# Every third low part of the weight units on GpSimd, from the differential heads' query projection to the first output projection

## The chip, the core and the metric

The kernel runs on one core of a Trainium2 chip. A core has five engines with queues of their own, each of which takes its instructions strictly in order: TensorE (PE in the profile, with its weight loads as PEld), VectorE (DVE), ScalarE (ACT), GpSimd (POOL) and SyncE (SP, which here only issues DMAs). The metric is the device time of one execution in microseconds; less is better. The time before is the median of three runs.

## The reference, cut to what matters

Two blocks of two layers each run on 256 tokens of width 1024. Only the first layer of the first block is touched by the change:

```
proj = h @ w_in                          # w_in: 1024 x 4096
qa, ka, va, qb, kb, vb, g = split(proj)  # 512 columns each, g has 1024
ya = dilated_mixture_attention(qa, ka, va)          # 8 heads
yb = differential_attention(qb, kb, vb, lam, ...)   # 4 heads, two softmaxes each
y  = concat(ya, yb) * silu(g)
x  = x + gate * (y @ w_out)              # w_out: 1024 x 1024
```

`gate` belongs to layer 0; `shift`, `scale` and `gate` of layer 1 are products of one vector `cs` with 1024 x 3072 weights (`ada_w`), and the kernel forms them during layer 0.

## The kernel before, in words

All matrix products are made in three passes on pairs of numbers: an f32 value is split into a high part, rounded to TensorE's reduced f32 format, and a low part, the rest. `mm3` (lines 245, 246, 247) issues the three matmuls high by high, low by high and high by low. The activations are split once. The weights are streamed: `unit` (line 224) loads 128 partitions by 1024 f32 (512 KB) into a raw tile `wr` by SP, ACT casts it to the high part `wh` (line 227), and DVE subtracts it from the raw tile to form the low part `wl` (line 228). There are 3 raw, 5 high and 5 low buffers (`NR, NH, NL`), so the load of the fourth unit from here waits until the `wl` of this one is formed, and SP, in order, holds all later loads behind it.

A projection of 512 columns takes four units, the output projection (`out_proj`) eight. In layer 0 the order is: qa, ka, va in two halves, twelve units; then the softmax of the `ya` heads (`scores_a`, `values_a`); then qb, kb, vb, the first half of the gate (`sgT_done`), the second half (columns 3584 on, below: the second gate projection), and the output projection, 28 units together. Softmax needs DVE on the path to TensorE: DVE adds bias to the scores in PSUM and takes the least (line 398), ACT exponentiates (401), DVE scales the probabilities (line 678 for `ya`, 731 for `yb`), TensorE transposes them (410). For `yb` GpSimd raises the variance to a power (`rstd`, line 337) and DVE applies it (751); at the end DVE multiplies `yb` by the gate (579) and TensorE transposes it (582) for the last half of the output projection.

Between all this lies the vector by matrix product for `ada_w`: `part` loads 256 KB pieces `aw` by SP (line 517), DVE multiplies and adds each into `macc` (462 for the first of eight, then 464), GpSimd adds one row of bias to one partition of `macc` (line 519), and TensorE sums over partitions (523).

The written order fixes priorities. A scheduler that runs when the program is built sets the order of the instructions on each engine, with costs of its own for each instruction. What an engine will do next is thus fixed before the run, and an instruction that isn't ready holds all behind it.

Of the kernel before, what the change touches and what calls it, by code (L numbers as in the profile page):

```python
# [9 lines left out]
F32 = mybir.dt.float32  # L10
# [89 lines left out]
class Net:  # L100
    def __init__(self, ctx, tc, a):
        self.tc, self.nc, self.a = tc, tc.nc, a
        p = lambda name, bufs, **k: ctx.enter_context(tc.tile_pool(name=name, bufs=bufs, **k))
        self.p_const = p("const", 1)
        self.p_raw = p("raw", NR)
        self.p_hi = p("whi", NH)
        self.p_lo = p("wlo", NL)
        self.p_act = p("act", 2)
        self.p_g = p("gat", 5)
        self.p_big = p("big", 2)  # L110
        self.p_ng = p("ng", 1)
        self.p_par = p("par", 3)
        self.ph = {}
        self.p_col = p("colp", 22)
        self.p_mm = p("mm", 4, space=PSUM)
        self.p_mx = p("mx", 4, space=PSUM)
        self.load_consts()
# [99 lines left out]
    def unit(self, src, shape, pieces=1):  # L217

        nc = self.nc
        raw = self.p_raw.tile([128, 1024], F32, name="wr", tag="raw")  # L220
        hi = self.p_hi.tile([128, 1024], F32R, name="wh", tag="hi")
        lo = self.p_lo.tile([128, 1024], F32R, name="wl", tag="lo")
        v = (lambda t: t) if len(shape) == 1 else v2
        nc.sync.dma_start(v(raw), src)
        m = 1024 // pieces
        for i in range(0, 1024, m):
            nc.scalar.copy(hi[:, i:i + m], raw[:, i:i + m])  # L227
            nc.vector.tensor_sub(lo[:, i:i + m], raw[:, i:i + m], hi[:, i:i + m].bitcast(F32))  # L228
        return v(hi), v(lo)

    def block(self, w, c0, k0=0, k1=8, pieces=1):
# [188 lines left out]
def v2(t):  # L420
    return t.rearrange("p (a b) -> p a b", a=2)
# [130 lines left out]
def gated_out(n, act, w, gate, after):  # L552
    nc = n.nc

    def done(t, j, ps):
        s = slice(j * 512, j * 512 + 512)
        tmp = n.g2("go")
        nc.vector.tensor_mul(tmp, ps, gate[:, s])
        nc.vector.tensor_add(n.x[:, t, s], n.x[:, t, s], tmp)
    n.out_proj(act, w, done, after)  # L560


def pipelined(items, first, second, lag=2, after=None):

    got = []
    for i in range(items + lag):
        if i < items:
            got.append(first(i))
        if i >= lag:
            second(i - lag, got[i - lag])  # L570
            if after:
                after(i - lag)
# [25 lines left out]
def even_layer(n, mod, later, follow):  # L598
    nc, a = n.nc, n.a
# [4 lines left out]
    def fm_done(name, scale):  # L604
        def done(i, ps):
            t = n.s2(name)
            if scale is None:
                nc.scalar.copy(t, ps)
            else:
                nc.scalar.activation(t, ps, AF.Copy, scale=scale)  # L610
            fm[name, i] = v2(t)
        return done
# [61 lines left out]
    def values_a(pr, got):  # L674
# [7 lines left out]
        ya[pr] = n.s2("ya", tag="yp")  # L682
        nc.scalar.copy(ya[pr], ps)
    pipelined(4, scores_a, values_a, 1, later)
    n.proj_fm(act, w, 1536, fm_done("qb", -0.125))
    n.proj_fm(act, w, 2048, fm_done("kb", None))
    n.proj_tok(act, w, 2560, tok_done("vb"))
# [77 lines left out]
        pair_out(n, yb[h], [sg[1, 0], sg[1, 1]], h * 128, yT, 4 + h)  # L765
    following = follow()
    gated_out(n, yT, a["ab_w_out"][0], mod.gate, following.tile)
    return following


# [103 lines left out]
def first_block(n):  # L874
    nc = n.nc
    c = n.ccol("c", 0, 8)
    cs = n.p_const.tile([128, 8], F32, name="cs")
    nc.scalar.activation(cs, c, AF.Tanh, scale=0.5)
    nc.vector.scalar_tensor_tensor(cs, cs, 1.0, c, op0=OP.add, op1=OP.mult)
    nc.vector.tensor_scalar(cs, cs, 0.5, None, op0=OP.mult)  # L880
    n.cs = cs
    n.csB = n.ng("csB")
    nc.vector.tensor_copy(n.csB.rearrange("p (a b) -> p a b", a=8), bc(cs.unsqueeze(2), [128, 8, 128]))
    mods = [Mod(n, 0)]

    todo = [(0, 2, 0), (0, 2, 1), (1, 1, 0), (1, 1, 1), (1, 0, 0), (1, 0, 1), (1, 2, 0), (1, 2, 1)]
    open_ = []

    def later(i):

        if open_:
            open_.pop()()
        if i == 2:
            mods.append(Mod(n, 1))
        if i < len(todo):
            m, part, half = todo[i]
            open_.append(mods[m].part(part, half))
    ada = even_layer(n, mods[0], later, lambda: AdaNorm(n, mods[1]))
    return odd_layer(n, ada.act, mods[1], lambda i: later(6 + i),
                     lambda: DoubleNorm(n, "norm1_g_2", 0, mods[1].gate)).act  # L900
# [844 lines left out]
```

## Time and profile before

| | |
|---|---|
| median of 3 runs | 1309.55 us (1307.87 to 1313.42) |
| the profiled execution | 1304.1 us, of which the span is 1302.3 us |
| PE busy | 95% of the span |
| DVE busy | 65% of the span, 120.28 of the 147.00 us from 60 to 207 us |
| ACT busy | 49% |
| POOL busy | 5% |

The span is cut by the profile's own clock from the first to the last instruction. Times of rows are microseconds from the start of the span. An engine's busy share says only how long it was at work; what it waited for stands beside a row in square brackets, as the idle time just before it and what ended it.

### The profile page before, as it was taken

Reading aid. Unit: us, or ns where it says so; the run is one execution under the profiler, and the core shown is the slowest. Engines: PE = TensorE matmul, PEld = TensorE weight load, DVE = VectorE, ACT = ScalarE, POOL = GpSimd, SP = SyncE. Lnnn points to the kernel's source line nnn. Section 1 sums busy time; section 2 is a strip of 40 time slices with the busy share of each in tenths; the row PEclk is TensorE's granted clock in tenths of the full one; section 3 lists DMA queues with packets and bytes.
Section 4 is the critical chain, followed back from the end, with each engine's and each line's share of the span. In section 5 each row is a group of like instructions: output and inputs, shape, how many; then the busy total and the mean of one; then the engine's idle time right before and its main releaser. Section 6 shows DMA issues by size and latency. Waiting matters only on the chain.

```text
span 1302.3 us, 21332 instructions
## 1 busy us (share of the span) xinstructions
PE 1240.6 (95%) x8352; PEld 1047.7 (80%) x8352; DVE 851.2 (65%) x1456; ACT 644.0 (49%) x1083; POOL 68.9 (5%) x82
## 2 busy tenths in 40 slices
PE   6889889999899999999999999999999999999997
PEld 3767667977787777887899987987787887999986
DVE  6977888676658755766755544668755757655543
ACT  3454645685655345444644433556345444544432
POOL 0021120000101000000000000010000000000000
PEclk8999999999999999999999999999999999999999
DMA  8988865654553233465666654753242564766552
GB/s 315 325 274 277 257 197 172 202 179 122 178 170 98 84 114 98 149 210 162 196 186 185 181 192 129 234 149 96 82 128 83 177 196 130 226 183 188 180 192 81
DMA packets 104960, 227.25 MB, mean 175 GB/s; under 512 B 8206, under 2 KB 8350, under 8 KB 104860
## 3 DMA queue, kind: packets, MB, share of 16 engines
q1 hardware_dynamic: 102560, 219.18, 54.0%
q0 software_dynamic: 1984, 6.60, 1.8%
q8 instruction: 65, 1.06, 0.3%
q14 instruction: 35, 0.29, 0.1%
q10 hardware_dynamic: 316, 0.12, 0.0%
HBM read 224.82 MB, written 1.05 MB: 173 GB/s over the span
## 4 chain that ended last, share of the span: by engine, by line
PE 70%; DVE 7%; issue 5%; ACT 3%; DMA 2%; POOL 1%; POOLq 0%; DVEq 0%; ACTq 0%; SPq 0%
PE mm L246 20%; PE mm L245 19%; PE mm L247 19%; PE p L369 2%; DVE wl L228 2%; PE hs L1156 1%; ACT wh L227 1%; PE sc L376 1%; PE px L1440 1%; PE tr L324 1%; DMA wr<-in_gu_dram 1%; PE pv L385 1%; PE cm L376 1%; PE pt L410 1%; PE pv L1002 1%
## 5 line engine op out<-in xcount | busy, mean ns | idle before, releaser
L228 DVE TENSOR_TENSOR wl<-wr,wh 128x1024 fp32r<-128x1024 f32 (+1 forms) x372 | 431.3, 1165 | 268.6 <-ACT wh L227 266.5
L227 ACT CAST wh<-wr 128x1024 fp32r<-128x1024 f32 (+1 forms) x372 | 369.7, 1002 | 396.7 <-PE mm L247 164.7
L245 PE MATMUL mm<-hh,wh 128*128 128x256 f32 x1168 | 332.1, 286 | 1.0 <-ACT hh L328 0.9
L247 PE MATMUL mm<-hh,wl 128*128 128x256 f32 x1168 | 332.7, 285 | 0.0
L246 PE MATMUL mm<-hl,wh 128*128 128x256 f32 x1168 | 332.3, 285 | 0.0
L245 PEld LDWEIGHTS mm<-hh,wh 128*128 128x128 f32 x1168 | 224.4, 193 | 3.7 <-ACT hh L328 1.9
L247 PEld LDWEIGHTS mm<-hh,wl 128*128 128x128 f32 x1168 | 224.5, 192 | 2.1 <-issue 1.9
L246 PEld LDWEIGHTS mm<-hl,wh 128*128 128x128 f32 x1168 | 224.6, 192 | 1.5 <-issue 1.2
L246 PE MATMUL mm<-wl,hh 128*128 128x512 f32 (+1 forms) x448 | 178.3, 398 | 1.5 <-DVE wl L228 1.5
L245 PE MATMUL mm<-wh,hh 128*128 128x512 f32 (+1 forms) x448 | 177.3, 396 | 0.9 <-DVE ropet L1069 0.4
L247 PE MATMUL mm<-wh,hl 128*128 128x512 f32 (+1 forms) x448 | 175.5, 392 | 0.4 <-DVE hl L329 0.3
L246 PEld LDWEIGHTS mm<-wl,hh 128*128 128x128 f32 x448 | 85.0, 190 | 19.7 <-DVE wl L228 2.4
L245 PEld LDWEIGHTS mm<-wh,hh 128*128 128x128 f32 x448 | 84.9, 190 | 18.7 <-ACT hh L328 1.2
L247 PEld LDWEIGHTS mm<-wh,hl 128*128 128x128 f32 x448 | 84.8, 189 | 17.0 <-DVE hl L329 1.4
L245 PE MATMUL mm<-wh,ff 128*128 128x512 f32 x176 | 69.5, 395 | 0.0
L246 PE MATMUL mm<-wl,ff 128*128 128x512 f32 x176 | 69.5, 395 | 0.0
L247 PE MATMUL mm<-wh,ff 128*128 128x512 f32 x176 | 69.4, 395 | 0.0
L464 DVE SCALAR_TENSOR_TENSOR macc<-aw,cs,macc 128x512 f32<-128x512 f32 x78 | 58.4, 762 | 11.9 <-DMA aw<-in_ada_w_dram 11.5
L401 ACT ACTIVATE p<-p,nm 128x256 f32<-128x256 f32 (+1 forms) x80 | 39.7, 497 | 32.0 <-DVE nm L398 29.2
L246 PE MATMUL mm<-wl,yTh 128*128 128x512 f32 x128 | 50.6, 396 | 1.1 <-DVE wl L228 1.1
L247 PE MATMUL mm<-wh,yTl 128*128 128x512 f32 x128 | 50.0, 390 | 0.0
L245 PE MATMUL mm<-wh,yTh 128*128 128x512 f32 x128 | 49.4, 395 | 0.1
(388 smaller groups left out, 1533.7 us busy)
## 6 DMA issues: line engine op xcount, KB each, us to landing
wr<-in_w_in_dram SPq DMA_DIRECT2D x120, 512.0 KB, 3.8
wr<-in_gu_dram SPq DMA_DIRECT2D x88, 512.0 KB, 3.7
wr<-in_w_ffn_down_dram SPq DMA_DIRECT2D x44, 512.0 KB, 3.3
aw<-in_ada_w_dram SPq DMA_DIRECT2D x80, 256.0 KB, 3.9
wr<-in_ab_w_in_dram SPq DMA_DIRECT2D x32, 512.0 KB, 5.3
wr<-in_c_w_in_dram SPq DMA_DIRECT2D x20, 512.0 KB, 4.4
wr<-in_w_branch_dram SPq DMA_DIRECT2D x16, 512.0 KB, 3.2
wr<-in_w_out_dram SPq DMA_DIRECT2D x16, 512.0 KB, 3.2
```

What stands on the lines that cost most here:

```text
L227: nc.scalar.copy(hi[:, i:i + m], raw[:, i:i + m])
L228: nc.vector.tensor_sub(lo[:, i:i + m], raw[:, i:i + m], hi[:, i:i + m].bitcast(F32))
L245: mm(out, lhsT=ah, rhs=bh, start=start, stop=False, **kw)
L246: mm(out, lhsT=ah, rhs=bl, start=False, stop=False, **kw)
L247: mm(out, lhsT=al, rhs=bh, start=False, stop=stop, **kw)
L324: nc.tensor.transpose(ps[:, j * 128:(j + 1) * 128], src[:, (g + j) * 128:(g + j + 1) * 128], self.ident)
L369: self.nc.tensor.matmul(out[r], lhsT=lhsT[:, r], rhs=rhs, **kw)
L376: mm = lambda out, lhsT, rhs: self.nc.tensor.matmul(out, lhsT=lhsT, rhs=rhs, start=True, stop=True)
L385: mm = lambda hh, kc: self.nc.tensor.matmul(ps[HALF[hh], :], lhsT=vs(hh, kc), rhs=pTs[hh][:, kc * 256:kc * 256 + 256], start=(kc == 0), st ...
L401: nc.scalar.activation(p, p, AF.Exp, bias=nm, scale=-1.0, accum_out=l)
L410: nc.tensor.transpose(ps[:, kc * 256 + t * 128:kc * 256 + t * 128 + 128], p[:, t, kc * 128:kc * 128 + 128], self.ident)
L464: nc.vector.scalar_tensor_tensor(acc, w, n.cs[:, k:k + 1], acc, op0=OP.mult, op1=OP.add)
```

## The change: which engine forms the low part

A counter `shared` runs while layer 0 goes from the projection of qb to the end of the output projection. It starts at 1 and goes 2, 3, 1, 2, 3 ...; whenever it is 3, GpSimd takes the subtraction instead of DVE. The second unit of the 28 is the first to go there, then every third: 9 units. Elsewhere nothing changes in the text. (Line numbers of the changed kernel are 1 to 6 higher: its line 230 is 228 here, 522 is 519, 467 is 464, 340 is 337.)

```
@@ __init__
         self.p_lo = p("wlo", NL)
+        self.shared = 0
@@ unit
             nc.scalar.copy(hi[:, i:i + m], raw[:, i:i + m])
-            nc.vector.tensor_sub(lo[:, i:i + m], raw[:, i:i + m], hi[:, i:i + m].bitcast(F32))
+            self.shared = self.shared and self.shared % 3 + 1
+            (nc.gpsimd if self.shared == 3 else nc.vector).tensor_sub(
+                lo[:, i:i + m], raw[:, i:i + m], hi[:, i:i + m].bitcast(F32))
@@ even_layer
     pipelined(4, scores_a, values_a, 1, later)
+
+    n.shared = 1
     n.proj_fm(act, w, 1536, fm_done("qb", -0.125))
...
     gated_out(n, yT, a["ab_w_out"][0], mod.gate, following.tile)
+    n.shared = 0
     return following
```

The scheduler then orders DVE, PE, ACT, SP and POOL anew within layer 0; behind it the order is as it was. Three places follow.

GpSimd's queue from the unpacking of the masks (`msk`) to the second `rstd`, first before and then in the changed kernel. `lv`, `G1`, `sub` and `sk` are DMAs that it issues itself.

```order
L519 TENSOR_TENSOR macc_760<-macc_760,adab_785 1x512
L519 TENSOR_TENSOR macc_850<-macc_850,adab_875 1x512
L167 DMA lv_1488<-in_rows_dram 128x64 x4
L167 DMA G1_940<-in_rows_dram 128x1024
L167 DMA sub_1498<-in_rows_dram 128x128
L519 TENSOR_TENSOR macc_944<-macc_944,adab_969 1x512
L519 TENSOR_TENSOR macc_1000<-macc_1000,adab_1025 1x512
L519 TENSOR_TENSOR macc_1602<-macc_1602,adab_1627 1x512
L167 DMA sk_2384<-in_rows_dram 128x16
L337 TENSOR_TENSOR rstd_1595<-var_1593,mhalf_97 128x2
L519 TENSOR_TENSOR macc_1693<-macc_1693,adab_1718 1x512
L337 TENSOR_TENSOR rstd_1686<-var_1684,mhalf_97 128x2
```

```order
L230 TENSOR_TENSOR wl_1158<-wr_1156,wh_1157 128x1024
L522 TENSOR_TENSOR macc_850<-macc_850,adab_875 1x512
...
L230 TENSOR_TENSOR wl_1176<-wr_1174,wh_1175 128x1024
L522 TENSOR_TENSOR macc_944<-macc_944,adab_969 1x512
L168 DMA sub_1498<-in_rows_dram 128x128
L230 TENSOR_TENSOR wl_1296<-wr_1294,wh_1295 128x1024
L522 TENSOR_TENSOR macc_1000<-macc_1000,adab_1025 1x512
...
L230 TENSOR_TENSOR wl_1826<-wr_1824,wh_1825 128x1024
L340 TENSOR_TENSOR rstd_1595<-var_1593,mhalf_97 128x2
L522 TENSOR_TENSOR macc_1693<-macc_1693,adab_1718 1x512
L340 TENSOR_TENSOR rstd_1686<-var_1684,mhalf_97 128x2
L230 TENSOR_TENSOR wl_1844<-wr_1842,wh_1843 128x1024
```

Each moved subtraction has come in among work of GpSimd that was there before; the one of `wl_1844` (the last unit of the second gate projection) stands right behind the second `rstd`, and two more follow later, the third and the sixth unit of the output projection.

DVE's queue at the end of the second gate projection, before and in the changed kernel. `wl_1940` and `wl_1958` are the first two units of the output projection, `yb_1808` is the last head, `sg` the gate, `macc_2976` the last accumulation of `ada_w` that is formed in layer 0.

```order
L335 TENSOR_SCALAR var_1816<-ss_1809 128x2
L228 TENSOR_TENSOR wl_1844<-wr_1842,wh_1843 128x1024
L751 SCALAR_TENSOR_TENSOR yb_1808<-pv_1807,rstd_1818,sub_1498 128x128 x2
L464 SCALAR_TENSOR_TENSOR macc_2976<-aw_2992,cs_123,macc_2976 128x512
L228 TENSOR_TENSOR wl_1940<-wr_1938,wh_1939 128x1024
L464 SCALAR_TENSOR_TENSOR macc_2976<-aw_2995,cs_123,macc_2976 128x512
L549 SCALAR_TENSOR_TENSOR sg_1896<-th_1897,mm_1822 128x512
...
L579 TENSOR_TENSOR yb_1808<-yb_1808,sg_1900 128x128
L228 TENSOR_TENSOR wl_1958<-wr_1956,wh_1957 128x1024
```

```order
L338 TENSOR_SCALAR var_1791<-ss_1784 128x2
L230 TENSOR_TENSOR wl_1940<-wr_1938,wh_1939 128x1024
...
L756 SCALAR_TENSOR_TENSOR yb_1808<-pv_1807,rstd_1818,sub_1498 128x128 x2
L467 SCALAR_TENSOR_TENSOR macc_2976<-aw_2992,cs_123,macc_2976 128x512
L230 TENSOR_TENSOR wl_1958<-wr_1956,wh_1957 128x1024
L467 SCALAR_TENSOR_TENSOR macc_2976<-aw_2995,cs_123,macc_2976 128x512
L552 SCALAR_TENSOR_TENSOR sg_1896<-th_1897,mm_1822 128x512
...
L582 TENSOR_TENSOR yb_1808<-yb_1808,sg_1900 128x128
L230 TENSOR_TENSOR wl_1994<-wr_1992,wh_1993 128x1024
```

`wl_1844` has left DVE, `wl_1940` now stands ahead of the last two heads, and `wl_1958` is formed ahead of the gating of the heads instead of behind it.

SP's queue in the same stretch, before and in the changed kernel. `wr_1974` and `wr_1992` are the raw tiles of the third and fourth unit of the output projection.

```order
L224 DMA wr_1956<-in_ab_w_out_dram 128x1024
L517 DMA aw_2894<-in_ada_w_dram 128x512
L517 DMA aw_2897<-in_ada_w_dram 128x512
...
L517 DMA aw_2995<-in_ada_w_dram 128x512
L517 DMA aw_2998<-in_ada_w_dram 128x512
L224 DMA wr_1974<-in_ab_w_out_dram 128x1024
L224 DMA wr_1992<-in_ab_w_out_dram 128x1024
```

```order
L225 DMA wr_1956<-in_ab_w_out_dram 128x1024
...
L225 DMA wr_1974<-in_ab_w_out_dram 128x1024
L520 DMA aw_2980<-in_ada_w_dram 128x512
...
L520 DMA aw_2995<-in_ada_w_dram 128x512
L225 DMA wr_1992<-in_ab_w_out_dram 128x1024
L520 DMA aw_2998<-in_ada_w_dram 128x512
L225 DMA wr_2010<-in_ab_w_out_dram 128x1024
```

The third unit of the output projection is now loaded six `aw` pieces before the point where it stood behind all of them.

## Rows read from the trace of the kernel before

**Rows 1.** The page: busy us, share of the span and instructions of each engine.

```profile
PE 1240.6 (95%) x8352; PEld 1047.7 (80%) x8352; DVE 851.2 (65%) x1456; ACT 644.0 (49%) x1083; POOL 68.9 (5%) x82
```

**Rows 2.** Busy time of each engine, 60 to 207 us, granted clock, DMA share.

```profile
60.00:207.00 147.00, 128.49 (x731) 100.94 (x729) 120.28 (x270) 76.84 (x172) 25.15 (x25) 0.97 0.80 253
```

**Rows 3.** What PE waited for, 60 to 207 us: total, times, longest.

```profile
PE pt L410 <- DVE p L731: 6.1, 3, 3.4
PE pt L410 <- DVE p L678: 5.7, 4, 2.8
PE sc L376 <- DVE nm L398: 2.9, 1, 2.9
PE mm L246 <- DVE wl L228: 2.3, 3, 1.2
```

**Rows 4.** What DVE waited for in the same stretch, longest first.

```profile
DVE macc L464 <- DMA aw<-in_ada_w_dram: 10.9, 12, 3.8
DVE wl L228 <- ACT wh L227: 5.5, 7, 1.2
```

**Rows 5.** Busy time of line 228 alone on DVE, from the projection of qb on.

```profile
61.50:201.00 139.50, 34.08 (x28) 0.96 0.81 254
```

**Rows 6.** GpSimd's own operations: line 519's shortest, median and longest ns; and a cast.

```profile
L519 POOL TENSOR_TENSOR macc<-macc,adab x8: 1271/1460/2152, 72.4 to 183.6; 1x512 f32<-1x512 f32 x8
...
57.75 0.92 POOL L194 CAST msk<-mskf 128x896 uint8<-128x896 f32 x1 [4.00 <-DMA mskf<-in_msk_dram]
```

**Rows 7.** DVE and GpSimd in order of time, where line 519 ran: start, us, engine.

```profile
70.98 0.35 DVE L678 TENSOR_SCALAR p<-p,rl 128x256 f32<-128x256 f32 x1
72.71 1.38 DVE L678 TENSOR_SCALAR p<-p,rl 128x256 f32<-128x256 f32 x1
...
124.16 1.22 DVE L228 TENSOR_TENSOR wl<-wr,wh 128x1024 fp32r<-128x1024 f32 x1
125.30 0.42 DVE L398 CUSTOM_DVE_ANT_0 p<-sc,bias 128x256 f32<-128x256 f32 x1
125.72 1.36 DVE L464 SCALAR_TENSOR_TENSOR macc<-aw,cs,macc 128x512 f32<-128x512 f32 x1
...
138.73 2.15 POOL L519 TENSOR_TENSOR macc<-macc,adab 1x512 f32<-1x512 f32 x1 [12.20 <-PE mm L247]
155.62 1.29 POOL L519 TENSOR_TENSOR macc<-macc,adab 1x512 f32<-1x512 f32 x1 [7.80 <-PE mm L247]
155.89 1.30 DVE L462 TENSOR_SCALAR macc<-aw,cs 128x512 f32<-128x512 f32 x1 [0.26 <-DMA aw<-in_ada_w_dram]
157.23 0.75 DVE L464 SCALAR_TENSOR_TENSOR macc<-aw,cs,macc 128x512 f32<-128x512 f32 x1
159.03 0.88 DVE L731 SCALAR_TENSOR_TENSOR p<-p,rl 128x256 f32<-128x256 f32 x2
169.18 1.89 DVE L731 SCALAR_TENSOR_TENSOR p<-p,rl 128x256 f32<-128x256 f32 x2
170.99 0.47 DVE L462 TENSOR_SCALAR macc<-aw,cs 128x512 f32<-128x512 f32 x1
```

**Rows 8.** The cast of `wr_1842`, GpSimd's second `rstd`, the subtraction, SP's next loads.

```profile
160.05 1.05 ACT L227 CAST wh<-wr 128x1024 fp32r<-128x1024 f32 x1 [2.00 <-PE mm L246]
160.06 0.70 POOL L337 TENSOR_TENSOR rstd<-var,mhalf 128x2 f32<-128x2 f32 x1 [3.16 <-DVE var L335]
177.32 1.22 DVE L228 TENSOR_TENSOR wl<-wr,wh 128x1024 fp32r<-128x1024 f32 x1
178.61 15.00 SPq L224 DMA_DIRECT2D wr<-in_ab_w_out_dram  x6
```

**Rows 9.** PE where it stood idle at the end of layer 0.

```profile
178.59 0.50 PE L246 MATMUL mm<-wl,hh 128*128 128x512 f32 x1 [1.18 <-DVE wl L228]
181.59 0.50 PE L246 MATMUL mm<-wl,yTh 128*128 128x512 f32 x1 [0.40 <-DVE wl L228]
187.63 0.50 PE L246 MATMUL mm<-wl,yTh 128*128 128x512 f32 x1 [0.67 <-DVE wl L228]
```

More of the change, by code (lines that the diff above doesn't have):

```diff
@@ L107, in __init__ @@
         self.p_lo = p("wlo", NL)
+        self.shared = 0
         self.p_act = p("act", 2)
@@ L227, in unit @@
             nc.scalar.copy(hi[:, i:i + m], raw[:, i:i + m])
-            nc.vector.tensor_sub(lo[:, i:i + m], raw[:, i:i + m], hi[:, i:i + m].bitcast(F32))
+            self.shared = self.shared and self.shared % 3 + 1
+            (nc.gpsimd if self.shared == 3 else nc.vector).tensor_sub(
+                lo[:, i:i + m], raw[:, i:i + m], hi[:, i:i + m].bitcast(F32))
         return v(hi), v(lo)
@@ L684, in even_layer @@
     pipelined(4, scores_a, values_a, 1, later)
+    n.shared = 1
     n.proj_fm(act, w, 1536, fm_done("qb", -0.125))
@@ L767, in even_layer @@
     gated_out(n, yT, a["ab_w_out"][0], mod.gate, following.tile)
+    n.shared = 0
     return following
```

## The prediction, as put on record before the run

> **What bounds the kernel now.** First the page: TensorE is busy 95% of the span and GpSimd 5% [rows 1], so over the whole kernel DVE looks like an engine with room. The change is confined to one stretch, so the second view is the busy time from 60 us, just before the first of the 28 units, to 207 us, where TensorE ends the output projection [rows 2]. There DVE is busy 120.28 of 147.00 us, 82%, and TensorE shows 128.49. TensorE is short of work, and the third view, what it waited for, says of whom: of DVE, 6.1 + 5.7 us for probabilities (`p`), 2.9 us for the least scores (`nm`), 2.3 us for a low part (`wl`), 17.0 us together [rows 3]. The reader is to see that DVE is late mostly with softmax, and that its queue is what makes it late: 28 subtractions of line 228 take 34.08 us of it [rows 5]. DVE itself waited 10.9 us for `aw` loads and 5.5 us for casts [rows 4]; in these gaps some lateness of DVE disappears. The most that the change could give back is thus the 17.0 us of TensorE's waits, and only part of it hangs on the nine subtractions.
>
> **The change part by part.** *Nine subtractions leave DVE.* One at 124.16 was followed by the next instruction at 125.30 [rows 7], so each frees 1.14 us, nine 10.3 us.
>
> *Nine come to GpSimd.* None of this shape ran there before, so its length has to be bounded. The nearest row is line 519, the same operation with two inputs in SBUF: 1.27 us at its shortest for 512 elements [rows 6]. Without any fixed part, 1024 elements take 2.54 us, the upper end. A cast with one input took 0.92 us for 896 elements, 1.03 ns each [rows 6]; two inputs one after the other are 2.06 ns, 2.1 us for 1024, the lower end. I take 2.4 us, nearer the same operation. The Trainium skill, "GPSIMD Engine Reference", section 3.1, gives 4497 ns for an add of 2048 f32, so an estimate of 2.25 us here; by it the term below would be nine times 0.15 us smaller at most.
>
> *What GpSimd's work does to DVE.* This is the disputed cost, and the trace of before shows it, because line 519 already runs among the same DVE work. While it ran, a `p` scaling of line 678 that takes 0.35 us took 1.38; an accumulation of line 464 took 1.36 us against 0.75; line 462 took 1.30 against 0.47; two of line 731 took 1.89 against 0.88; and while the one at 138.73 ran, nothing on DVE was stretched [rows 7]. DVE lost 1.03, 0.61, 0.83, 1.01 and 0 us, 0.70 us in the mean, of 1.27 us. The bias step at 125.30, which reads scores in PSUM, kept its 0.42 us, though GpSimd was under way. So what is held up is DVE's work on tiles in SBUF, among it the subtractions that stay. GpSimd is held up in turn: the one at 138.73 took 2.15 us where 1.27 is possible.
> For a run of 2.4 us the loss lies between the same share, 0.70 / 1.27 x 2.4 = 1.32 us, and the same free lead ahead of the first instruction that is held, 2.4 - (1.27 - 0.70) = 1.83 us. With nothing to choose between them I take the middle, 1.58 us; nine times that is 14.2 us. DVE, meant to be relieved, is 14.2 - 10.3 = 3.9 us later. Of this the share in which DVE is busy, 82%, is carried on, and the rest falls into its gaps: **+3.2 us**.
>
> *The end of layer 0.* This is where the new order gives something back. The raw tile `wr_1842` was cast at 160.05, but its low part was formed only at 177.32 on DVE; the load that needs its buffer, and all behind it, left at 178.61 [rows 8]. In the changed kernel GpSimd forms it behind the second `rstd`, which ran at 160.06 [rows 8]. Ready at 161.1, it would be done by 164.7 even after a wait of 1.2 us, so the buffer comes free some 13 us sooner, and SP has moved the third unit of the output projection ahead of six `aw` loads. TensorE waited 1.18 us for this low part, then 0.40 for the output projection's first and 0.67 for its second [rows 9], both of which now come earlier on DVE. These three, 2.25 us, should go: **-2.2 us**. The gating of the heads itself comes no sooner: as many subtractions stand ahead of it on DVE as before, since `wl_1958` has taken the free place.
>
> *Edits that I cost at nothing.* GpSimd's queue: the nine stand beside line 519, `rstd` and DMAs, and nothing behind them is short of time unless they run late; cover is GpSimd's idleness, 25.15 us of 147 busy [rows 2]. If it were gone, the `rstd` behind `wl_1826` would come up to 2.4 us late, with two heads' normalisation behind it on DVE. ACT does the same casts, and DMA the same bytes. Layers after the first keep their order, so what is won or lost by 207 us goes straight to the end.
>
> *Sum.* +3.2 - 2.2 = +1.0 us on the profiled execution's 1304.1, so 1305.1. That execution lies 0.42% below the median of the three runs (1309.55 / 1304.1 = 1.0042), so in terms of the median 1310.5 us. Half a percent, 6.5 us, is about what a measurement of this kernel can tell from no change; +1.0 is far within.
>
> **The rivals.** *Slower, by GpSimd holding DVE for its whole length.* If every run of 2.4 us meets DVE with an instruction that needs SBUF, DVE loses 9 x 2.4 - 10.3 = 11.3 us; 82% is +9.3, and the gated heads then come so late that the 2.2 us at the end aren't won: 1313.4, or 1318.9 in terms of the median. For it speak four of five events in rows 7, in which the held instruction waited until GpSimd was done; against it the bias steps, reciprocals and gaps that lie between. It turns the sign from a loss of (10.3 + 2.2 / 0.82) / 9 = 1.44 us each, and it is over 0.5% only from 2.3 us each with the end still won, or 2.0 with it lost. The Trainium skill, "SBUF — State Buffer", section "Who interferes with whom", states it as a rule: of a GpSimd instruction and a DVE instruction with two inputs in SBUF the later one is blocked for the whole length of the other; and "Perfetto Trace Analysis", section "Optimizing Scalar/DVE Operations", warns that moving work between the two may not help. The trace agrees that the whole length is held (155.62 + 1.29, and line 462 is done 0.28 us later); how often it is met decides.
>
> *Faster, because the runs fall where DVE has nothing to lose.* As at 138.73: if the loss is half of what rows 7 show, 0.70 us of each 2.4, DVE gains 10.3 - 6.3 = 4.0 us, 82% is 3.3, with the end 5.5 us less; with no loss at all 0.82 x 10.3 + 2.2 = 10.6 us less. So 1293.5 to 1298.6, in terms of the median 1299 to 1304, and the shorter waits for `p` lie on TensorE's way. For it: DVE waits for `aw` 12 times [rows 4], and a held `aw` accumulation costs TensorE nothing at once. Against it: four of five events.
>
> *DVE's lateness never arrives.* If DVE's waits for `aw` and casts (16.4 us in rows 4) take it all, only the end is left: -2.2, 1301.9, in the median's terms 1307.3.
>
> *GpSimd in order, the low part late.* A moved subtraction waits behind line 519, which waits for its own accumulation. Then TensorE, which waited three times for a low part, waits 2.4 - 1.14 = 1.3 us longer for some: at nine 11.3 us, likelier two or three, 3 us, on top of +1.0: 1308.1, or 1313.5. The order speaks against more, since most of the nine stand ahead of the line 519 beside them. That the change doesn't take place is excluded: the order has nine subtractions on GpSimd.
>
> **How the numbers follow.** Forecast as summed 0.40, lateness hidden 0.12, GpSimd in order 0.10, all of these within 0.5%, save a tenth of their sum, which I give to slower; held throughout 0.13; faster 0.25, about as much as the favourable part of the loss's bounds (0 to 2.4 us, with the mean seen in their lower half by share and in the upper half by lead). That makes faster 0.25, same 0.56, slower 0.19. The range: the fastest case's upper part and the slowest case's lower one, 1302 to 1317, leaves out some 2 in 10. The likeliest case alone: 1307 to 1313.
>
> **What the profile after would show.** Nine rows of line 230 on POOL of 2.1 to 2.6 us when free, longer where they start inside a subtraction. On DVE, accumulations and `p` scalings stretched by 1 to 2 us beside them, and the sum of these stretches near 14 us; if it is under 7, the faster rival holds; near 21, the slower. Waits of TensorE for `p` should stand near 12 to 15 us. The 1.18, 0.40 and 0.67 us at the end of layer 0 should be gone, and the third unit of the output projection loaded about 13 us sooner. The end of the output projection should lie within 4 us of 207, and everything after it shifted as one. I am wrong if a subtraction on GpSimd takes over 3 us on its own, if the new order moves TensorE's waits for softmax by more than the lock does, or if `aw` loads, not DVE, set the pace throughout.

## The result, and the profile after

Slower: a median of 1320.17 us over five runs (1318.33 to 1320.86) against 1307.87 (1304.18 to 1313.42), ratio 1.0089, 95% interval 1.0069 to 1.0108, so about +11.6 us. That is outside the range of the prediction. Each kernel was timed beside runs of before of its own; in what follows its ratio to them is turned into us on 1307.

The page's first part of the kernel after, which answers to [rows 1], then its line for the stretch (busy us and number of instructions of PE, PEld, DVE, ACT and POOL, then granted clock and DMA), which answers to [rows 2], from 60 us to the first `var` of the next normalisation at 218.91 us, and the same line for before, where that `var` stands at 205.75:

```profile
PE 1251.2 (95%) x8352; PEld 1054.5 (80%) x8352; DVE 854.0 (65%) x1447; ACT 644.9 (49%) x1083; POOL 91.6 (7%) x91
...
60.00:218.91 158.91, 135.40 (x720) 105.65 (x719) 120.83 (x256) 74.93 (x165) 49.21 (x35) 0.89 0.74 236
```

```profile
60.00:205.75 145.75, 127.31 (x727) 100.30 (x726) 119.48 (x268) 75.59 (x169) 24.21 (x24) 0.96 0.80 252
```

The event is 13.2 us later, and the rest of the program is shifted by 14 to 16 us. DVE's work has not shrunk (119.48 to 120.83 us) although nine subtractions left it. TensorE's busy time grew by 8.1 us and its idle time by 5.1 (from 145.75 - 127.31 = 18.4 to 158.91 - 135.40 = 23.5); its granted clock in the stretch fell from 0.96 to 0.89.

What TensorE waited for in the same stretch, against [rows 3], and DVE, against [rows 4]:

```profile
PE pt L413 <- DVE p L736: 5.5, 4, 2.0
PE pt L413 <- DVE p L681: 3.1, 2, 2.4
PE sc L379 <- ACT kb L611: 2.5, 1, 2.5
PE mm L248 <- DVE sg L552: 2.2, 1, 2.2
PE sc L379 <- DVE nm L401: 2.1, 1, 2.1
PE pv L388 <- ACT pT L415: 1.9, 1, 1.9
...
DVE macc L467 <- DMA aw<-in_ada_w_dram: 14.2, 9, 4.5
DVE wl L230 <- ACT wh L228: 7.4, 4, 3.4
```

The waits for `p` are shorter than before (8.6 against 11.8 us); new ones have come beside them, for ACT (`kb`, the copy of the keys, and `pT`) and for the gate `sg`. None of TensorE's waits was ended by a low part of GpSimd's. Next the GpSimd rows of the moved subtraction (duration in ns: least, median, longest), DVE's accumulations of line 467, which answer to line 464 of before, and one meeting of the two in order of time; [rows 6, 7] answer:

```profile
L230 POOL TENSOR_TENSOR wl<-wr,wh x9: 2382/2599/2966, 68.4 to 204.9; 128x1024 fp32r<-128x1024 f32 x9
...
L467 DVE SCALAR_TENSOR_TENSOR macc<-aw,cs,macc 128x512 f32<-128x512 f32 x54 | 50.5, 934 | 14.7 <-DMA aw<-in_ada_w_dram 14.2
...
82.84 2.69 POOL L230 TENSOR_TENSOR wl<-wr,wh 128x1024 fp32r<-128x1024 f32 x1 [8.96 <-ACT wh L228]
82.53 3.54 DVE L467 SCALAR_TENSOR_TENSOR macc<-aw,cs,macc 128x512 f32<-128x512 f32 x2
85.99 0.15 DVE L671 RECIPROCAL rl<-l 128x1 f32<-128x1 f32 x1
```

Two accumulations that take about 1.4 us take 3.54: the second ends half a microsecond after GpSimd does (82.84 + 2.69 = 85.53). In before the same 54 accumulations took 40.9 us:

```profile
L464 DVE SCALAR_TENSOR_TENSOR macc<-aw,cs,macc 128x512 f32<-128x512 f32 x54 | 40.9, 757 | 11.0 <-DMA aw<-in_ada_w_dram 10.9
```

For all kernels below I work out one number in the same way, the **held time**: the duration of every DVE instruction from 60 to 250 us (some 300) less the median of its kind (line, operation, shape) in the trace of before, summed, less the same sum of before itself (4.4 us). It comes from one execution of each kernel, and changes by up to 1.6 us with the way in which neighbouring instructions are grouped. For the kernel after it is 12.6 us; 9.6 of it is the difference between the two rows of accumulations above (50.5 against 40.9).

The end of layer 0, where TensorE stood idle, for [rows 9], and, for [rows 8], the cast of `wr_1842`, its low part on GpSimd and the load behind it, of the third unit of the output projection:

```profile
194.76 0.50 PE L249 MATMUL mm<-wl,yTh 128*128 128x512 f32 x1 [0.55 <-DVE wl L230]
198.13 0.49 PE L248 MATMUL mm<-wh,yTh 128*128 128x512 f32 x1 [2.17 <-DVE sg L552]
212.39 0.73 PE L248 MATMUL mm<-wh,yTh 128*128 128x512 f32 x2 [0.49 <-ACT wh L228]
213.65 0.50 PE L249 MATMUL mm<-wl,yTh 128*128 128x512 f32 x1 [0.30 <-DVE wl L230]
...
175.41 1.05 ACT L228 CAST wh<-wr 128x1024 fp32r<-128x1024 f32 x1
176.54 2.97 POOL L230 TENSOR_TENSOR wl<-wr,wh 128x1024 fp32r<-128x1024 f32 x1 [5.08 <-ACT wh L228]
179.53 0.33 SPq L225 DMA_DIRECT2D wr<-in_ab_w_out_dram  x1
```

The cast came at 175.41 where before has 160.05, so the load left at 179.53, no sooner than in before (178.61).

### The profile page after: what moved, and what is told of

Same layout as the page of the kernel before. It is cut to its first block, busy times and chain, and to the rows that moved or that the text cites. A ratio compares the mean times of both kernels' runs of the same rounds, so it can differ in the third digit from the quotient of the medians.

```text
span 1318.4 us, 21330 instructions
## 1 busy us (share of the span) xinstructions
PE 1251.2 (95%) x8352; PEld 1054.5 (80%) x8352; DVE 854.0 (65%) x1447; ACT 644.9 (49%) x1083; POOL 91.6 (7%) x91
## 4 chain that ended last, share of the span: by engine, by line
PE 69%; DVE 7%; issue 5%; ACT 3%; DMA 2%; POOL 2%; DVEq 0%; POOLq 0%; ACTq 0%
PE mm L249 19%; PE mm L250 19%; PE mm L248 19%; PE p L372 2%; DVE wl L230 2%; PE hs L1162 1%; ACT wh L228 1%; PE sc L379 1%; DMA wr<-in_gu_dram 1%; PE px L1446 1%; PE pv L388 1%; DMA aw<-in_ada_w_dram 1%; PE cm L379 1%; PE pv L1008 1%; PE pt L413 1%
## 5 line engine op out<-in xcount | busy, mean ns | idle before, releaser
L230 DVE TENSOR_TENSOR wl<-wr,wh 128x1024 fp32r<-128x1024 f32 (+1 forms) x363 | 421.1, 1167 | 272.0 <-ACT wh L228 269.0
L248 PEld LDWEIGHTS mm<-wh,hh 128*128 128x128 f32 x448 | 84.7, 189 | 18.4 <-ACT hh L331 1.2
L467 DVE SCALAR_TENSOR_TENSOR macc<-aw,cs,macc 128x512 f32<-128x512 f32 x78 | 67.4, 877 | 15.7 <-DMA aw<-in_ada_w_dram 14.9
```

Source lines behind the costliest of these rows:

```text
L230: (nc.gpsimd if self.shared == 3 else nc.vector).tensor_sub(lo[:, i:i + m], raw[:, i:i + m], hi[:, i:i + m].bitcast(F32))
L248: mm(out, lhsT=ah, rhs=bh, start=start, stop=False, **kw)
L467: nc.vector.scalar_tensor_tensor(acc, w, n.cs[:, k:k + 1], acc, op0=OP.mult, op1=OP.add)
```

## The experiments

Theories. **L**: GpSimd's reading holds DVE up, and TensorE waits for what DVE makes. **O**: the new order of the work, which the scheduler makes of other costs, moves TensorE's waits. **R** (added after the first four runs): taking work from DVE, with the order that comes of it, gives nothing here. **C**: part of the time is TensorE at its lower clock, whatever starts it. In the table, "order" names the kernel whose rows TensorE, DVE, ACT and SP have, in its order ("before's" but for two to four matmuls of 8352). Kernels with "DVE relieved" don't form the low parts of the moved units at all.

| Kernel | what GpSimd adds | order | held, us | us against before (95%) |
|---|---|---|---|---|
| after | 9 subtractions | its own | +12.6 | +11.6 (9.0 to 14.1) |
| e4_extra | 18 reads of 512 | before's | +10.4 | +9.3 (5.9 to 12.6) |
| e10_twice | 36 reads of 512 | before's | +22.6 | +22.3 (19.6 to 25.0) |
| e13_reads_first | 8 reads, first four units | before's | +3.4 | +2.9 (1.3 to 4.4) |
| e14_reads_last | 10 reads, last five | before's | +5.4 | +7.7 (5.2 to 10.3) |
| e9_write | 45 memsets | before's | +0.1 | -0.7 (-2.7 to 1.3) |
| e6_pieces | 36 subtractions of 256 | after's | +7.7 | +9.5 (6.5 to 12.5) |
| e5_memset | 18 memsets, DVE relieved | nearly after's | +0.4 | +2.0 (0.0 to 3.8) |
| e11_skip | nothing, DVE relieved | nearly after's | -0.7 | -1.0 (-2.9 to 0.7) |
| e3_act | nothing, DVE relieved | its own | -1.0 | -0.7 (-2.6 to 1.4) |
| e1_first12 | 4 subtractions | its own | +7.7 | +11.6 (8.4 to 14.9) |
| e15_skip_first | nothing, DVE relieved | e1's | +0.1 | +6.3 (4.6 to 8.0) |
| e2_last16 | 5 subtractions | its own | +5.1 | +6.8 (4.3 to 9.3) |
| e16_skip_last | nothing, DVE relieved | nearly e2's | -0.8 | -4.1 (-5.9 to -2.2) |
| e7_u20 | 1 subtraction | its own | +1.5 | +2.1 (0.1 to 4.1) |
| e8_double | nothing, DVE gets more | its own | +0.7 | +6.4 (3.9 to 8.9) |
| e12_macc | 8 additions fewer | its own | -6.7 | +1.2 (-0.8 to 3.1) |
| e17_later5 | nothing | its own | +0.1 | -2.1 (-4.1 to -0.1) |

### Holds alone, in before's order

**e4_extra**, against before, for every third unit:

```diff
+                d = self.p_scr.tile([128, 512], F32, name="scr", tag="scr")
+                for j in range(0, 1024, 512):
+                    nc.gpsimd.tensor_sub(d, hi[:, j:j + 512].bitcast(F32), hi[:, j:j + 512].bitcast(F32))
```

> All subtractions stay on VectorE as before; for each of the nine units GpSimd also does two subtractions of 512 elements (hi minus hi) into a tile that nobody reads. The rows of TensorE, VectorE, ScalarE and SyncE keep the order of the kernel before. Theory L (GpSimd's subtractions hold up VectorE's operations, and TensorE waits for those): nearly the whole loss comes without any work being moved; VectorE's rows beside the extra ones grow by some 10 us in sum, as in the changed kernel, and the time is 1316 to 1322. Theory O (the loss comes from the new order in which the work is issued): 1306 to 1311, and TensorE's pauses in the stretch from 60 us to the end of the first output projection stay as before even where VectorE's rows grow. Theory C (the loss is time at TensorE's lower clock, whatever starts it): the time follows the number of windows with a granted clock under 0.95 in the stretch, 3 of them in 1308, about 9 in 1320; C is beside L or O, not against them.

+9.3 us, with no work moved: L without O. Since the order is before's, the two traces can be laid over each other, up to the same `var`: first its stretch from the DVE instruction that stands at 60.00 in before (59.73), then from the matmul that stands there (62.86), since TensorE was 26 matmuls further back when the stretch began; the 15 us behind its longest wait; its GpSimd rows and its accumulations, and two of TensorE's waits:

```profile
59.73:219.16 159.43, 134.13 (x753) 105.87 (x752) 130.65 (x268) 76.77 (x169) 50.12 (x44) 0.94 0.73 235
62.86:219.16 156.30, 131.00 (x727) 102.74 (x726) 129.60 (x267) 75.58 (x167) 49.20 (x43) 0.93 0.72 233
141.34:156.34 15.00, 13.56 (x62) 10.22 (x63) 11.98 (x25) 7.39 (x18) 5.64 (x5) 0.84 0.67 211
...
L235 POOL TENSOR_TENSOR scr<-wh 128x512 f32<-128x512 f32 x18 | 24.9, 1382 | 35.0 <-ACT wh L229 34.4
L471 DVE SCALAR_TENSOR_TENSOR macc<-aw,cs,macc 128x512 f32<-128x512 f32 x54 | 44.2, 818 | 9.8 <-DMA aw<-in_ada_w_dram 9.4
...
141.34 0.48 PE L417 MATMUL pt<-cst,p 128*128 128x128 f32 x1 [4.87 <-DVE p L740]
180.72 0.48 PE L417 MATMUL pt<-cst,p 128*128 128x128 f32 x1 [2.64 <-DVE p L740]
```

```profile
134.37:149.37 15.00, 14.60 (x71) 10.95 (x71) 12.22 (x30) 7.92 (x20) 3.85 (x3) 0.89 0.78 242
...
134.37 0.42 PE L410 MATMUL pt<-cst,p 128*128 128x128 f32 x1 [3.36 <-DVE p L731]
170.73 0.33 PE L410 MATMUL pt<-cst,p 128*128 128x128 f32 x1 [1.28 <-DVE p L731]
```

The second fence is before. A wait of 3.36 us became 4.87, one of 1.28 became 2.64. Over the stretch DVE was busy 11.2 us longer for the same 268 instructions (130.65 - 119.48). For the same 727 matmuls TensorE took 10.6 us more (156.30 against 145.75): 6.9 are idle time (18.4 to 25.3) and 3.7 are busy time (127.31 to 131.00). The granted clock of the stretch was 0.93 against 0.96, and in the 15 us behind the longer wait 0.84 against 0.89, that is, more of it passed at the lower level, 1.2 GHz. So C holds beside L: a hold is paid as waiting and, for a third of the time here, as TensorE's slower work.

**e10_twice** (four reads for each unit) and **e9_write** (one read of two columns, then five memsets, for each unit):

```diff
-                for j in range(0, 1024, 512):
+                for j in (0, 512, 0, 512):
```
```diff
+                nc.gpsimd.tensor_sub(d[:, 0:2], hi[:, 0:2].bitcast(F32), hi[:, 0:2].bitcast(F32))
+                for j in range(5):
+                    nc.gpsimd.memset(d, 0.0)
```

> e4_extra with four subtractions of 512 elements on GpSimd for each of the nine units in place of two; the order on the other engines is that of the kernel before. Theory L: the price goes with the GpSimd time that reads beside VectorE; e4_extra cost 9 us, so twice the dose costs 16 to 20: 1322 to 1328. If only the first meeting of each unit counts: 1315 to 1319.

> All subtractions stay on VectorE as before; behind each of the nine high parts GpSimd does one subtraction of two columns (so that it starts where the extra work of e4_extra starts) and five memsets of 512 columns, which write and read nothing, into a tile that nobody reads. The other engines keep the order of the kernel before. If what costs is that GpSimd reads SBUF beside VectorE (theory L as e4_extra left it), nearly nothing is left: 1306 to 1311. If any GpSimd work there costs, because its queue keeps macc, rstd or transfers of its own waiting (rival Q), 1314 to 1320, as with e4_extra.

Twice the reads: 22.6 us held, +22.3. TensorE's stretch for the same 727 matmuls:

```profile
60.91:230.68 169.77, 137.36 (x727) 108.45 (x726) 141.36 (x268) 75.64 (x168) 73.03 (x59) 0.89 0.69 215
```

Of its 24.0 us more, 10.1 are busy time, at a granted clock of 0.89. Memsets of the same total length: nothing held, nothing lost. GpSimd's rows of e9_write, and DVE's accumulations beside them:

```profile
L236 POOL MEMSET scr<- 128x512 f32 x45 | 24.2, 538 | 2.5
...
L472 DVE SCALAR_TENSOR_TENSOR macc<-aw,cs,macc 128x512 f32<-128x512 f32 x54 | 41.3, 765 | 10.3 <-DMA aw<-in_ada_w_dram 10.1
```

24.2 us of writing left line 472 at 765 ns (757 before); 24.9 us of reading put it at 818. GpSimd's queue as such costs nothing. The Trainium skill, "SBUF — State Buffer", section "Who interferes with whom", says that a DVE instruction with two inputs in SBUF meets a GpSimd instruction that reads SBUF and not one that only writes; the two rows agree.

**e13_reads_first** and **e14_reads_last** are e4_extra with the counter of units stopped behind the value projection, or started there.

> e4_extra's reading of high parts by GpSimd for the first four units alone, in the order of the kernel before. If the place decides (holds in the softmax stretch cost more): most of e4_extra's 9 us, 1313 to 1316. If a held microsecond costs 0.9 everywhere: about 4 us, 1309 to 1312.

> e4_extra's reading for the last five units alone, in the order of the kernel before. If the place decides: 1306 to 1309. If a held microsecond costs 0.9 everywhere: about 5 us, 1310 to 1313. With e13 it should add up to 9 us.

+2.9 for 3.4 us held, +7.7 for 5.4: a held microsecond costs 0.85 in the first stretch and 1.4 in the second, though the intervals (0.4 to 1.3 and 1.0 to 1.9) overlap. My guess that the first four carry most is refuted. What TensorE waited for longest in e14_reads_last, 60 to 220 us:

```profile
PE pt L417 <- DVE p L740: 9.9, 4, 4.8
PE pt L417 <- DVE p L685: 4.4, 4, 2.6
```

The differential heads' `p` (line 740, 731 before) went from 6.1 to 9.9 us; the other heads' (line 685, 678 before) did not grow, 5.7 to 4.4.

**e6_pieces**, after with `for j in range(i, i + m, 256)` around the GpSimd subtraction:

> The changed kernel with each GpSimd subtraction cut into four of 256 elements; the order on the other engines is that of the changed kernel. Theory L: each hold is at most a quarter as long, some 0.6 to 0.7 us, but VectorE meets up to four of them; if one hold meets one VectorE operation, the loss falls by about three quarters (1309 to 1313); if every piece is met, it stays (1318 to 1322). Theory O: 1317 to 1323, unless the pieces alone are slower than one whole by more than 1 us, which puts it above.

+9.5 with 7.7 us held: less is held, with pieces of 953 ns, 3.8 us a unit in place of 2.6. The interval reaches after's +11.6, so this run doesn't tell the theories apart.

### Relief without holds

**e11_skip**, against after, with no work in the place of the nine subtractions, and **e3_act**, **e5_memset**:

```diff
-            (nc.gpsimd if self.shared == 3 else nc.vector).tensor_sub(
-                lo[:, i:i + m], raw[:, i:i + m], hi[:, i:i + m].bitcast(F32))
+            if self.shared == 3:
+                lo = self.last
+            else:
+                nc.vector.tensor_sub(lo[:, i:i + m], raw[:, i:i + m], hi[:, i:i + m].bitcast(F32))
+        self.last = lo
```
```diff
+                nc.scalar.copy(lo[:, i:i + m], raw[:, i:i + m])
```
```diff
+                nc.gpsimd.memset(raw, 0.0)
+                nc.gpsimd.memset(lo.bitcast(F32), 0.0)
```

> The changed kernel with the nine GpSimd subtractions taken out and nothing in their place: the products of these units take the low part of the unit before (their own low parts are left out). VectorE is relieved of nine subtractions, GpSimd does nothing more than before, and the order on TensorE is near that of the changed kernel. Step (a) of the prediction, with its weight of 0.82: 8 us less than before, 1298 to 1301. Theory R (the relief is worth nothing, since VectorE waits longer for transfers of aw and for ScalarE's high parts instead, as the run with ScalarE copies has it): 1305 to 1310.

> Neither VectorE nor GpSimd forms the nine low parts: ScalarE copies raw into them (the subtraction of these nine units is left out). GpSimd has no added work. Theory L: VectorE is relieved of 10.3 us without any hold, ScalarE gets nine rows of about 1.1 us; 1300 to 1309. Theory O: an order different from both kernels, and so a number of pauses that neither has; 1308 to 1322 is open, and its TensorE pauses in the stretch say which. Theory C: time goes with the granted clock of the stretch, as in the others.

> Each of the nine GpSimd subtractions is replaced by two GpSimd memsets (of raw and of the low part), which only write; the low part of these nine units is left out (zeros). The order of the work on the other engines is nearly that of the changed kernel. Theory L: VectorE's rows beside the memsets don't grow, VectorE is relieved of nine subtractions (10.3 us), and the time is 1300 to 1309. Theory O: the order is as after, so the time is 1316 to 1322, with the same pauses of TensorE for rows that ScalarE, VectorE and GpSimd's macc rows end. Theory C: the granted clock of the stretch follows the time, 0.89 at 1320 and 0.97 at 1308.

-1.0, -0.7 and +2.0: R. With the order that comes of it, taking nine subtractions from DVE is worth nothing in three different forms. Each has a new order, and no run has the relief in before's, so relief and order aren't parted here. The window and the waits of e11_skip in the stretch (60 to 206 us):

```profile
60.00:206.20 146.20, 128.70 (x729) 102.81 (x728) 108.08 (x258) 75.36 (x166) 23.42 (x25) 0.94 0.79 255
...
PE sc L383 <- ACT kb L615: 4.8, 1, 4.8
PE sc L383 <- DVE nm L405: 3.4, 1, 3.4
PE pv L392 <- ACT pT L419: 3.0, 1, 3.0
PE pt L417 <- DVE p L740: 2.2, 1, 2.2
PE pt L417 <- DVE p L685: 1.4, 1, 1.4
...
DVE macc L471 <- DMA aw<-in_ada_w_dram: 18.4, 11, 3.7
```

DVE was busy 11.4 us less (119.48 to 108.08) and the stretch is as long as before (146.20 and 145.75): DVE's own wait for `aw` grew from 10.9 to 18.4 us. The relief did reach TensorE: its waits for `p` fell from 11.8 to 3.6 us. But it was idle for 17.5 us against 18.4, since it now waits for ACT's `kb` and `pT`, 7.8 us that before doesn't have. How `kb` came to be late, and the same place on ACT in before:

```profile
126.00 0.75 DVE L471 SCALAR_TENSOR_TENSOR macc<-aw,cs,macc 128x512 f32<-128x512 f32 x1 [1.48 <-DMA aw<-in_ada_w_dram]
126.90 2.10 POOL L526 TENSOR_TENSOR macc<-macc,adab 1x512 f32<-1x512 f32 x1 [16.55 <-DVE macc L471]
129.03 0.23 ACTq L487 DMA_DIRECT2D adab<-in_rows_dram  x1
129.31 1.07 ACT L615 COPY kb<-mm 128x512 f32<-128x512 f32 x2 [5.13 <-POOL macc L526]
129.94 1.38 PE L383 MATMUL sc<-kb,qb 64*128 64x256 f32 x6 [4.83 <-ACT kb L615]
```

```profile
123.57 0.58 ACT L608 COPY kb<-mm 128x512 f32<-128x512 f32 x1
126.56 0.23 ACTq L480 DMA_DIRECT2D adab<-in_rows_dram  x1
```

ACT issues the load of the next bias row (`adab`), which here waits for GpSimd's addition to `macc`, and that one for DVE's accumulation and its `aw` load. In before the copies of `kb` stand ahead of this load on ACT, here behind it. It is so in all kernels in which the first four units leave DVE; TensorE's wait for `kb` is 1.8 to 4.8 us in them, and none in the others.

After against e11_skip is the price of its holds in nearly the same order: +12.7 us for 13.3 held. e5_memset, whose order is nearer to after's, gives 9.7 for 12.2.

**e8_double** is e4_extra with `nc.vector` for `nc.gpsimd`:

> The kernel before with two more subtractions of 512 elements on VectorE for each of the nine units (hi minus hi, into a tile that nobody reads): VectorE gets some 11 to 12 us of work that it does itself, where in e4_extra it lost about as much to holds. The order of TensorE's rows changes in a few places. If VectorE's time has one price, whoever takes it (0.7 to 0.8): 1315 to 1319. If work in VectorE's own order is placed where it has slack, as the worthless relief says, and a hold strikes what is on the path: 1306 to 1312.

```profile
L235 DVE TENSOR_TENSOR scr<-wh 128x512 f32<-128x512 f32 x18 | 12.3, 685 | 0.1
```

+6.4 for 12.3 us of DVE's own work, 0.5 a microsecond, but in an order of its own, so only roughly between the two expectations.

### Selections of units

**e1_first12** has `n.shared = 0` behind the value projection, **e2_last16** has `n.shared = 1` only there; **e15_skip_first** and **e16_skip_last** are the same two with e11_skip's edit.

> Only the four units of the query, key and value projections of the differential heads go to GpSimd; the five behind them stay on VectorE. Theory L with a price that is the same everywhere (10 to 12 us over nine): 1312 to 1314. If most of the loss is in this stretch, where TensorE waits for the softmax, as the growing distance between the two traces has it (some 8 of 14 us by 118 us): 1315 to 1318. If the softmax stretch can hide it, 1306 to 1310.

> Only the five units from the first gate projection on go to GpSimd. Theory L with one price everywhere: 1313 to 1316. If the first four carry most of the loss: 1309 to 1313. With e1_first12 it adds up to the changed kernel's loss of 12 us if holds are independent of each other; if the sum is well over that, the two stretches share waits.

> e1_first12 without its four GpSimd subtractions, and with the low part of the unit before in the place of theirs (their own low parts are left out); the order on the other four engines is the same row for row. If the order alone costs something: 1309 to 1312, and the four holds the rest of e1_first12's 11.6 us. If the order costs nothing: 1304 to 1308, and four holds of 7.7 us in sum cost 11.

> e2_last16 without its five GpSimd subtractions, in the same way (the low parts of five units are left out); its order is near that of e2_last16. If the holds make up that kernel's 6.8 us: 1304 to 1308. If the order does: 1309 to 1313.

e1 and e2 together cost 18.4 us, after 11.6. e15 and e16 part the holds from the rest: e1 is +6.3 by order and relief and 5.4 by 7.6 us held; e2 is -4.1 by order and relief and 10.9 by 5.9 held (in an order only near its own). So order and relief together are no small thing for a single selection, from -4 to +6; for the nine together they are -1.0 (e11). That the later stretch costs more for each held microsecond comes out here again (0.7 and 1.8).

**e7_u20** moves the unit at the end of the second gate projection alone:

> One unit alone goes to GpSimd, the last of the second gate projection, behind which the kernel before has the three waits of TensorE for low parts (2.25 us in sum). If step (d) of the prediction holds without the other eight holds: 1304 to 1308, one hold of 1.4 us against 2.2 us less of waiting. If relief of VectorE is worth nothing, as e3_act has it: 1308 to 1311.

+2.1 (0.1 to 4.1), against -0.8 by the prediction's own terms (1.4 for the hold, 2.2 won). Here the low part was early and the third unit's load left when it should:

```profile
166.16 0.38 SPq L225 DMA_DIRECT2D wr<-in_ab_w_out_dram  x1
```

That is 12.5 us sooner than in before, and the three waits for low parts are gone, but TensorE waited 1.6 us each for `sg` and a cast and 1.5 for ACT's `yb` in their place.

### Two attempts at a faster kernel

**e12_macc**, line 519 of before on DVE (`nc.gpsimd.tensor_add` to `nc.vector.tensor_add`):

> The kernel before, with the eight additions of a 1x512 row to macc (line 519, 1589 ns each on GpSimd) on VectorE. In the trace of before, five of them lie beside VectorE rows that are 4.2 us longer than their kind. If these holds cost what the added ones cost (9 us for some 12 of holding): about 3 us gained, less what eight rows of about 0.5 us cost VectorE: 1303 to 1307. If VectorE's new rows take as much, or the new order does: 1306 to 1311.

```profile
L519 DVE TENSOR_TENSOR macc<-macc,adab 1x512 f32<-1x512 f32 x8 | 5.4, 671 | 0.0
```

The holds that before has are gone (-6.7 us), DVE has 5.4 us more of its own in another order, and the time is the same.

**e17_later5**, all on DVE, the subtractions of the last five units of e2_last16 issued later:

```diff
+            with self.lazily(1000 if self.shared == 3 else 0):
+                nc.vector.tensor_sub(lo[:, i:i + m], raw[:, i:i + m], hi[:, i:i + m].bitcast(F32))
```

> The kernel before, with the subtractions of the last five units still on VectorE, but placed later in its order, behind ready work of other kinds; nothing is left out. If e16_skip_last's gain comes from the order in which TensorE's softmax work stands (its 4 us less than before): 1302 to 1306. If it comes from five subtractions less on VectorE: 1306 to 1310.

1304.98 us against 1308.01, ratio 0.9984 (0.9969 to 0.9999): the one version that does all the work and is below both kernels, by so little that it is barely told from no change. It is an order of its own and not e16_skip_last's, so where the 4 us there come from stays open.

## Why the prediction was wrong

**Right in mechanism and size: GpSimd's length and the holds.** 2.38 us at the shortest against my 2.4, and 12.6 us held against 14.2 (1.40 each against 1.58). That a held instruction waits until GpSimd is done fits the row at 82.53. GpSimd's queue costs nothing, as costed (e9_write), and no low part of GpSimd's kept TensorE waiting. DMA was not tested apart.

**The step that failed: the netting of relief against holds**, "DVE, meant to be relieved, is 14.2 - 10.3 = 3.9 us later", times 0.82, +3.2. It gave a microsecond taken from DVE and one added by a hold the same price, and it put the new order at nothing but the end of layer 0. Measured: relief and new order together are worth 1.0 us, not 0.82 x 10.3 + 2.2 = 10.6 (e11_skip, with e3_act and e5_memset); a held microsecond costs 0.89 to 0.99 in before's order (e4_extra, e10_twice) and 0.95 in after's (after against e11_skip; 0.8 against e5_memset). With e11_skip's -1.0 and the prices of before's order the step reads -1.0 + (0.89 to 0.99) x 13.3 = +10.8 to +12.2, around the +11.6 measured. The share of time in which DVE is busy is thus about right as a price of holds, a little low, and wrong for relief. What took the relief in e11_skip is in its trace: TensorE's waits for `p` fell by 8.2 us, and 7.8 us of waits for ACT's `kb` and `pT` came, `kb` because its copy now stands behind a load that hangs on `aw`. That `aw` loads set a pace was in [rows 4], and I used it only as a rival for lateness. How much of the +7.8 is the order and how much would have shown in any order wasn't parted.

**The clock wasn't in the sum.** I counted holds as waits alone. In e4_extra 3.7 of the 10.6 us are TensorE's busy time, at a lower granted clock; in e10_twice 10.1 of 24.0. After and e11_skip, for the same 778 matmuls:

```profile
60.25:234.62 174.37, 148.19 (x778) 114.51 (x777) 135.39 (x281) 83.54 (x181) 51.26 (x38) 0.90 0.70 224
61.31:221.92 160.61, 140.41 (x778) 110.63 (x777) 121.59 (x281) 82.66 (x181) 24.45 (x27) 0.95 0.74 239
```

Here it is 7.8 of 13.8. These are shares in single profiled executions.

**The end of layer 0, -2.2**: not won. The step let the cast of `wr_1842` stay at 160.05; in the kernel after it came at 175.41, so the low part was done at 179.51 and not at 164.7, and the third unit's load left 0.9 us later than in before, where I had 13 sooner. Of the waits for low parts 0.85 us is left (0.55 and 0.30), but one of 2.17 us for `sg` came. Nor did it pay where the load did come sooner: e7_u20, with this unit alone, is +2.1.

**Views that I named as tests.** Held time "near 14": right. Waits for `p` of 12 to 15 us: wrong, 8.6. The end within 4 us of 207: wrong, it came 13 us later. The third unit loaded 13 us sooner: wrong, as said. "If the new order moves the waits by more than the lock does": in the time it did not for the nine together (-1.0 with the relief, against +12.7), though TensorE's waits moved by some 8 us. The rival "held for the whole length" forecast 1318.9, near the result, by another sum: it has 21.6 us held, and 12.6 were.

**Open.** Why a held microsecond costs about twice as much in the later stretch; the waits show for whom (`p` of the differential heads), not why. What makes the -4 of e16_skip_last, and all but the `kb` of e15_skip_first's +6. e12_macc's nothing fits holds and DVE work of one price, unlike e11_skip; its order differs, and it was not taken apart.

## What to carry to other kernels

Relief of an engine and a hold on it are two prices, not one: relief is worth only what isn't then spent waiting for something else, here for copies on ACT that the new order put behind a load, and a hold strikes whatever is next, here at nearly full price. Measure them apart: the same order with the extra work added into a scratch tile gives the hold, the work left out gives the relief, with the order that comes of it. When two traces are laid over each other, begin at the same instruction of each engine. Before work goes from DVE to GpSimd, ask whether it reads SBUF, and whether DVE's work there is on the way to TensorE.

## What the runs showed of the hardware

- GpSimd's reading and writing differ wholly for DVE: 24.9 us of subtractions held DVE for 10.4 us and cost 9.3 (e4_extra), 24.2 us of memsets 0.1 and nothing (e9_write).
- One GpSimd subtraction of 1024 elements took 2.6 us beside DVE, four of 256 took 4 x 0.95 = 3.8 in all (e6_pieces); whether a piece has a large fixed part, or DVE held each of them up, was not separated.
- Of what a late DVE cost, a third to a half was TensorE's busy time at a lower granted clock: 3.7 us of 10.6 for the same matmuls (e4_extra), 10.1 of 24.0 (e10_twice).
- The order that the scheduler makes of a small change is worth, with four or five subtractions less on DVE, +6 and -4 us in this stretch (e15_skip_first, e16_skip_last).
- A copy on ACT that stood behind a DMA issue waited with it: ACT idle 5.13 us, TensorE 4.83 (e11_skip).
